# A hybrid decoder layer: the expert layers spread over the gate steps in another order, and chunk order at three stage borders

## The chip, the cores and the metric

The kernel runs on one core of a Trainium2 chip. The metric is the device time of one execution, in microseconds (us).

## What is computed

One decoder layer on 512 tokens of width 1024, in float32: two token mixers side by side (sparse attention and a state-space scan), a cross-attention to 256 memory tokens, and a PEER channel mixer, with a norm ahead of each. The change touches the cross-attention and PEER:

```python
h = h + merged @ w_out
h = h + memory_cross_attention(rmsnorm(h), rmsnorm(mem), w_cross_q, w_cross_kv, w_cross_out)
h = h + peer_ffn(rmsnorm(h), ...)
...
def peer_ffn(a, w_q, sub_keys, u_tab, v_tab):     # 8 heads, 128 keys a side, 16384 experts
    s = scores of both half queries against 128 sub keys
    s_top, i_top = top_k(s, 16)                   # per head and half
    sc, ci = top_k(all 256 sums, 16)              # 16 experts of each head
    gw = softmax(sc)
    act = gelu(a . u_tab[experts])
    return sum(gw * act * v_tab[experts])         # 128 experts a token
```

## The kernel before, in words

A tile framework records the program and a scheduler orders the instructions of each engine by their dependences, buffers and priorities. So the order on an engine is not the order of the code, and a tile's number of buffers decides how far loads and casts run ahead. All large products are made from a high and a low float32r part of each operand: `mm3` (L140) issues hi times hi, hi times lo for each of the eight chunks of the inner dimension, and then lo times hi for all chunks. `split` (L87) makes the parts: a cast on ScalarE (L90) and a subtraction (L91) on VectorE or GpSimd.

PEER runs for three blocks of 128 tokens (384, "dense") through all 16384 experts as 128 layers of 128 experts. Layer 1 (`layer1`, L890) is Gelu(uT a): 24 matmuls of 384 columns. Layer 2 (`layer2`, `sum_up`) multiplies by the gate weight of each token and expert and sums over vtab. The fourth block of tokens gathers its 128 experts' rows by indirect DMA on GpSimd (`gather_u`, `gather_v`; tile gr) and uses VectorE.

- *Choices* (`project` L949, `head` L968): for each of eight heads TensorE makes the scores (ps_q, ps_s) and VectorE the two rounds of top 16 with indices. `keep_some(n)` (L897) puts n layers of layer 1 between; their results, of which there are N_KEPT = 76, are stored to DRAM (gd) for later. `gather_some(P1G, h)` (L932) starts two gathers behind each block of a head and multiplies those started earlier.
- *Softmax* over the 16 scores of a head (L1046 to L1054), then eight layers (L1056).
- *Gate steps* (L1084 to L1115): 24 steps, eight for each of three blocks of tokens. `turned(b)` (L1062) transposes a block's chosen rows, columns and weights (ps_e). A step makes four one-hot operands on VectorE (oa, ob, obh, obl), 32 small matmuls (ps_w) that turn them into the gate weights of all 16384 experts for 16 tokens, four copies on ScalarE (stg) and a store to DRAM (wd). Behind the matmuls stands `keep_some`: two layers in the first two steps, one in the others.
- *Layer 2 stage*: gate weights (W) and the stored layer-1 results (gk) are loaded back, the rest of layer 1 is run, and yo is summed.

While the choices run, the weights of layer 1 are loaded into a ring of four buffers (cr), before and after into one of two (ur); the cast parts uh and ul have two buffers each. The loads stand on SP's queue, one behind another.

Of the kernel before, what the change touches and what calls it, by code (L numbers as in the profile page):

```python
# [21 lines left out]
T = 512  # L22
D = 1024
KC = 8
# [27 lines left out]
N_KEPT = 76  # L52
DENSE = 384
NTB = DENSE // 128
TG = 16
A8 = 8
P1G, P2G = 2, 0
NEARLY = 2
DELAY = 3


# [1 line left out]
def tile_hybrid(ctx, tc, xT, memT, pos, prm, cst, win, wab, wsb, wou, wcq, wckv, wco, wpq, subk, uT, utab, vtab,  # L63
# [73 lines left out]
                V.tensor_tensor(lo, raw, hi.bitcast(F32), op=OP.subtract)  # L137
        return hi, lo

    def mm3(ps, w, xh, xl, n=T, m=128, first=True, last=True, late_xl=False):  # L140

        hi, lo = w
        a, b, c = (hi, xh), (hi, xl), (lo, xh)
        order = [(*p, k) for k in range(KC) for p in (a, b)] + [(*c, k) for k in range(KC)]
        if late_xl:
            order = [(*p, k) for p in (a, c, b) for k in range(KC)]
        for i, (w_, x_, k) in enumerate(order):
            TE.matmul(ps[:m, :n], w_[:, k, :m], x_[:, k, :n], start=first and i == 0,  # L148
                      stop=last and i == len(order) - 1)
# [24 lines left out]
    def rsqrt_bc(ss, n, width):  # L174

        return bcast(rsqrt_small(const, ss[:, :n // 128], n // 128, 1.0 / width), n)
# [31 lines left out]
    ss = psum("ac", "ss")  # L208
# [499 lines left out]

    def mem_kv(m):
        ps = psum("mm", "ps_kv")  # L710
        mm3(ps, wtile(wckv[m], V if m < 12 else G), meH, meL, n=256)
        if m < 8:
            S.copy(kkT[:, m, :], ps[:, :256])
        else:
            vT = gen("vvT")[:, :256]
            S.copy(vT, ps[:, :256])
            ps2 = psum("sm", "ps_vv")
            for i in range(2):
                TE.transpose(ps2[:, i * 128:(i + 1) * 128], vT[:, i * 128:(i + 1) * 128], ident)
            V.tensor_copy(kkv[:, m - 8, 256:512], ps2[:, :256])  # L720
# [32 lines left out]
    for m in range(8):  # L753
        xr = gen("xr")
        SY.dma_start(xr, xT[:, m, :])
        ps = psum("mm", "ps_o")
        mm3(ps, wtile(wou[m]), mH, mL)
        V.tensor_tensor(h1[:, m, :], ps, xr, op=OP.add)
        S.activation(cH[:, m, :], h1[:, m, :], AF.Copy, scale=pc("g_cross", m))
        V.scalar_tensor_tensor(cL[:, m, :], h1[:, m, :], pc("g_cross", m), cH[:, m, :].bitcast(F32),  # L760
                               op0=OP.mult, op1=OP.subtract)
        if m < 7:
            add_square(sh, h1[:, m, :], T, m == 0)
        else:
            sum_small(ss, sh, T, True, False)
            sum_small(ss, square(h1[:, m, :], T), T, False, True)
    rs = wk.tile([128, T], F32, name="rs_c", bufs=1)
    S.copy(rs, rsqrt_bc(ss, T, D))

    for m in range(12, 14):  # L770
        mem_kv(m)


    xH, xL = slot2("xH", R), slot2("xL", R)
# [32 lines left out]
    sh = const.tile([128, T], F32, name="sh2", tag="rsf")  # L807
    for m in range(8):
        ps = psum("mm", "ps_h2")
        mm3(ps, wtile(wco[m]), xH, xL)  # L810
        V.tensor_tensor(h1[:, m, :], h1[:, m, :], ps, op=OP.add)
        if m < 7:
            add_square(sh, h1[:, m, :], T, m == 0)
        else:
            sum_small(ss, sh, T, True, False)
            sum_small(ss, square(h1[:, m, :], T), T, False, True)
# [152 lines left out]
    def head(h, sS, before):  # L969
# [3 lines left out]
        for b in order:  # L973
            for p in range(2):
                s = sS[:, p, b, :]
                V.max(out=tv[:, b, p, 0:8], in_=s)
                V.max_index(ti[:, b, p, 0:8], tv[:, b, p, 0:8], s)
                V.match_replace(out=s, in_to_replace=tv[:, b, p, 0:8], in_values=s, imm_value=TAKEN)
                V.max(out=tv[:, b, p, 8:16], in_=s)
                V.max_index(ti[:, b, p, 8:16], tv[:, b, p, 8:16], s)  # L980
            keep_some(2 if b == order[0] else 1)
            if b == order[0] and before is not None:
                decode(h - 1, *before)
            gather_some(P1G if h < 7 else 0, h)


        ca = sp.tile([128, 4, 64], F32, name="ca", tag="ca")
# [65 lines left out]
    V.tensor_tensor(sw, sw, top[:, :, None].to_broadcast([128, 32, 16]), op=OP.mult)  # L1053
    V.tensor_copy(gwt, slW[:, 3, :])  # L1054

    keep_some(8)  # L1056
    se1.close()
    choosing[0] = False
    vp = ctx.enter_context(tc.tile_pool(name="vp", bufs=1, side="right", reuse_waits="tile"))
# [21 lines left out]
        return eT  # L1081

    nxt = turned(0)
    for b in range(NTB):  # L1084
        eT = nxt
        for g in range(128 // TG):
# [13 lines left out]
            V.tensor_tensor(ob, io, bc(1), op=OP.is_equal)  # L1100
            V.tensor_tensor(obh, ob, bc(2), op=OP.mult)
            V.tensor_tensor(obl, ob, bc(3), op=OP.mult)
            for q in range(TG // 4):
                ps = psum("sm", "ps_w")
                for i in range(4):
                    w_ps, at_ = ps[:, i * 128:(i + 1) * 128], (slice(None), (q * 4 + i) // 2, slice(None), i % 2)
                    TE.matmul(w_ps, obh[at_], oa[at_], start=True, stop=False)  # L1107
                    TE.matmul(w_ps, obl[at_], oa[at_], start=False, stop=True)  # L1108
                S.activation(stg[:, :, q * 4:q * 4 + 4].rearrange("b a t -> b t a"),
                             ps.rearrange("b (t a) -> b t a", t=4), AF.Copy, scale=1.0 / 32768)  # L1110
            S.dma_start(wd[b * (128 // TG) + g], stg.rearrange("b a t -> b (a t)"))
            keep_some(2 if b * 8 + g < NEARLY else 1)
            gather_some(P2G)
    keep_some(N_KEPT)
    se2.close()  # L1115

# [221 lines left out]
```

## Time and profile before

| | before |
|---|---|
| median of 3 runs | 2165.53 us (2162.18 to 2165.95) |
| profiled execution | 2165.43 us |
| its span in the trace | 2163.7 us |
| TensorE busy | 2103.3 us (97% of the span) |
| VectorE busy | 1596.5 us (74%) |
| ScalarE busy | 977.6 us (45%) |
| GpSimd busy | 562.8 us (26%) |
| chain that ended last | PE 82%, DVE 12%, DMA 2%, ACT 2% |

The profiled execution lies by 1.7 us above its own span and within the runs. The names in the profile are PE (TensorE), PEld (its weight loads), DVE (VectorE), ACT (ScalarE), POOL (GpSimd) and SP. A busy share is an average over stages that are bound by different engines, so the stretches are read one by one below. A time in brackets behind a row is the idle time of the engine just before it, and what ended it.

### The profile page before, as it was taken

How to read it: one execution, taken by the hardware profiler on the slowest of the kernel's cores; microseconds unless marked ns; L12 is line 12 of the kernel's file. 1: busy time of each engine (PE TensorE's matmuls, PEld its weight loads, DVE VectorE, ACT ScalarE, POOL GpSimd, SP SyncE). 2: the span in 40 equal slices, each digit the busy share in tenths (PEclk: the TensorE clock that was granted, in tenths of full speed). 3: DMA queues.
4: the chain of work that ended last, by engine and by line, in shares of the span. 5: the costliest groups of instructions: out<-in, count | busy, mean ns of one | idle time of the engine just before them, and what ended most of it. 6: DMA issues, size and time to landing. Idle time of an engine off the chain costs nothing.

```text
span 2163.7 us, 29945 instructions
## 1 busy us (share of the span) xinstructions
PE 2103.3 (97%) x11045; PEld 1816.1 (84%) x11045; DVE 1596.5 (74%) x3018; ACT 977.6 (45%) x1513; POOL 562.8 (26%) x348
## 2 busy tenths in 40 slices
PE   9999999999999999999999999999999999999998
PEld 7888788777887877798988899988888888888887
DVE  6877855579943434589999588578778878788886
ACT  4453356666622434343434477633333333333333
POOL 0000000144134423214231000034344444444430
PEclk9999999999999999999999999999999999999999
DMA  4433332476453323258776376899999999999982
GB/s 138 136 108 116 104 103 83 126 209 181 143 165 103 121 68 107 98 168 308 262 240 223 130 259 257 287 329 370 324 331 337 336 354 327 350 319 332 339 304 79
DMA packets 209138, 469.27 MB, mean 217 GB/s; under 512 B 16064, under 2 KB 109376, under 8 KB 205792
## 3 DMA queue, kind: packets, MB, share of 16 engines
q1 hardware_dynamic: 152832, 284.10, 40.8%
q0 software_dynamic: 36864, 134.23, 16.8%
q10 hardware_dynamic: 19296, 49.03, 5.9%
q8 instruction: 86, 1.41, 0.3%
q14 instruction: 60, 0.49, 0.1%
HBM read 416.64 MB, written 50.66 MB: 216 GB/s over the span
## 4 chain that ended last, share of the span: by engine, by line
PE 82%; DVE 12%; DMA 2%; ACT 2%; issue 1%; POOL 0%; SPq 0%; DVEq 0%; ACTq 0%
PE yo L1144 24%; PE ps_u L148 19%; PE ps_in L148 16%; PE pss L148 4%; PE ps_cq L148 2%; PE ps_h L148 2%; DVE gr L908 2%; DVE ul L91 2%; PE ps_o L148 2%; PE psa L148 1%; PE ps_q L148 1%; PE ps_kv L148 1%; PE ps_w L1107 1%; PE ps_w L1108 1%; PE po L559 1%
## 5 line engine op out<-in xcount | busy, mean ns | idle before, releaser
L148 PE MATMUL ps_u<-fH,uh 128*128 128x384 f32 x1024 | 352.1, 344 | 12.0 <-ACT uh L90 12.0
L148 PE MATMUL ps_u<-fL,uh 128*128 128x384 f32 x1024 | 347.8, 340 | 0.0
L906 POOL DMA_INDIRECT gr<-utab,gidx x128 | 186.0, 1453 | 581.6 <-DVE gr L908 464.4
L91 POOL TENSOR_TENSOR wl<-wr,wh 128x1024 fp32r<-128x1024 f32 x60 | 148.1, 2469 | 661.5 <-PE ps_in L148 409.2
L919 POOL DMA_INDIRECT gr<-vtab,gidx x128 | 189.7, 1482 | 241.5 <-DVE acc L923 216.6
L90 ACT CAST vh<-vr 128x1024 fp32r<-128x1024 f32 x128 | 134.5, 1051 | 221.1 <-PE yo L1144 165.9
L90 ACT CAST wh<-wr 128x1024 fp32r<-128x1024 f32 x132 | 138.4, 1048 | 165.6 <-PE ps_in L148 78.5
L148 PE MATMUL ps_u<-fH,ul 128*128 128x384 f32 x1024 | 201.6, 338 | 8.2 <-DVE ul L91 8.0
L148 PEld LDWEIGHTS ps_u<-fH,uh 128*128 128x128 f32 x1024 | 196.4, 192 | 15.2 <-ACT uh L90 13.0
L148 PE MATMUL ps_in<-aH,wh 128*128 128x512 f32 x520 | 208.0, 400 | 0.0
L148 PE MATMUL ps_in<-aL,wh 128*128 128x512 f32 x520 | 204.7, 394 | 0.0
L1144 PE MATMUL yo<-vh,mh 128*128 128x512 f32 x768 | 199.8, 394 | 3.2 <-ACT mh L1134 3.2
L1144 PE MATMUL yo<-vh,ml 128*128 128x512 f32 x768 | 199.2, 393 | 0.0
L1144 PE MATMUL yo<-vl,mh 128*128 128x512 f32 x768 | 198.4, 392 | 0.0
L148 PEld LDWEIGHTS ps_u<-fL,uh 128*128 128x128 f32 x1024 | 196.4, 192 | 1.9
L91 DVE TENSOR_TENSOR vl<-vr,vh 128x1024 fp32r<-128x1024 f32 x128 | 156.6, 1225 | 55.1 <-ACT vh L90 44.2
L91 DVE TENSOR_TENSOR ul<-ur,uh 128x1024 fp32r<-128x1024 f32 x82 | 103.3, 1262 | 124.1 <-ACT uh L90 63.3
L148 PEld LDWEIGHTS ps_u<-fH,ul 128*128 128x128 f32 x1024 | 180.1, 189 | 12.7 <-DVE ul L91 12.7
L1144 PEld LDWEIGHTS yo<-vh,ml 128*128 128x128 f32 x768 | 145.1, 189 | 31.9
L1144 PEld LDWEIGHTS yo<-vl,mh 128*128 128x128 f32 x768 | 144.7, 188 | 31.8
L1144 PEld LDWEIGHTS yo<-vh,mh 128*128 128x128 f32 x768 | 144.2, 189 | 31.5 <-ACT mh L1134 3.5
L923 DVE SCALAR_TENSOR_TENSOR acc<-gr,gwt,acc 128x1024 f32<-128x1024 f32 x127 | 163.1, 1284 | 0.8
(472 smaller groups left out, 4066.5 us busy)
## 6 DMA issues: line engine op xcount, KB each, us to landing
vr<-vtab SPq DMA_DIRECT2D x128, 512.0 KB, 6.5
ur<-uT SPq DMA_DIRECT2D x80, 512.0 KB, 4.8
wr<-win SPq DMA_DIRECT2D x71, 512.0 KB, 3.6
cr<-uT SPq DMA_DIRECT2D x48, 512.0 KB, 4.3
wd<-stg ACTq DMA_DIRECT2D x24, 1024.0 KB, 4.0
W<-wd SPq DMA_DIRECT2D x16, 1536.0 KB, 14.3
gd<-ga ACTq DMA_DIRECT2D x76, 192.0 KB, 3.1
gk<-gd SPq DMA_DIRECT2D x76, 192.0 KB, 5.1
```

The lines of the kernel that those rows point to most:

```text
L90: made_hi[0] = S.copy(hi, src)
L91: return (lo_eng or V).tensor_tensor(lo, src, hi.bitcast(F32), op=OP.subtract)
L148: TE.matmul(ps[:m, :n], w_[:, k, :m], x_[:, k, :n], start=first and i == 0, stop=last and i == len(order) - 1)
L559: TE.matmul(po[:, b * 128:(b + 1) * 128], vt[:, s, (h // 4) * 128:(h // 4 + 1) * 128], pt[:, s * 128:(s + 1) * 128], start=s == 0, stop=s ...
L906: G.indirect_dma_start(out=r[:], out_offset=None, in_=utab[:, :], in_offset=bass.IndirectOffsetOnAxis(ap=gidx[:, k:k + 1], axis=0))
L908: return lambda: V.scalar_tensor_tensor(r, r, 1.0, afg, op0=OP.mult, op1=OP.mult, accum_out=gdot[:, k:k + 1])
L919: G.indirect_dma_start(out=r[:], out_offset=None, in_=vtab[:, :], in_offset=bass.IndirectOffsetOnAxis(ap=gidx[:, k:k + 1], axis=0))
L923: return lambda: V.scalar_tensor_tensor(acc, r, gwt[:, k:k + 1], acc, op0=OP.mult, op1=OP.add)
L1107: TE.matmul(w_ps, obh[at_], oa[at_], start=True, stop=False)
L1108: TE.matmul(w_ps, obl[at_], oa[at_], start=False, stop=True)
L1144: TE.matmul(yo[b][i], m[:, b * 128:(b + 1) * 128], v[:, i * 512:(i + 1) * 512], start=a == seq[0] and p == 0, stop=a == seq[-1] and p == 2)
```

## The change

Four things change.

1. `mm3` gets `late_k`: the three products of one chunk stand together, chunk by chunk. It is used for the first output block of three products: the memory keys, the output projection and the cross output.
2. Behind the cross norm's sum, one memory product (`mem_kv(12)`) stands between the inverse root and its broadcast.
3. No gathers are started behind the last block of a head in the choices; instead one is started in every second gate step.
4. Behind the softmax stands one layer instead of eight (`LAST1`), then the first transposes. In each gate step the layers stand ahead of the matmuls of the one-hots: two in the first step, then 29 spread over 23 steps (one each, two in six of them). Four layers stand behind the last step (`LAST2`).

```diff
@@ -54,8 +54,8 @@
 NTB = DENSE // 128
 TG = 16
 A8 = 8
-P1G, P2G = 2, 0
-NEARLY = 2
+P1G = 2
+LAST1, LAST2 = 1, 4
 DELAY = 3
 
 
@@ -137,13 +137,15 @@
                 V.tensor_tensor(lo, raw, hi.bitcast(F32), op=OP.subtract)
         return hi, lo
 
-    def mm3(ps, w, xh, xl, n=T, m=128, first=True, last=True, late_xl=False):
+    def mm3(ps, w, xh, xl, n=T, m=128, first=True, last=True, late_xl=False, late_k=False):
 
         hi, lo = w
         a, b, c = (hi, xh), (hi, xl), (lo, xh)
         order = [(*p, k) for k in range(KC) for p in (a, b)] + [(*c, k) for k in range(KC)]
         if late_xl:
             order = [(*p, k) for p in (a, c, b) for k in range(KC)]
+        if late_k:
+            order = [(*p, k) for k in range(KC) for p in (a, b, c)]
         for i, (w_, x_, k) in enumerate(order):
             TE.matmul(ps[:m, :n], w_[:, k, :m], x_[:, k, :n], start=first and i == 0,
                       stop=last and i == len(order) - 1)
@@ -708,7 +710,7 @@
 
     def mem_kv(m):
         ps = psum("mm", "ps_kv")
-        mm3(ps, wtile(wckv[m], V if m < 12 else G), meH, meL, n=256)
+        mm3(ps, wtile(wckv[m], V if m < 12 else G), meH, meL, n=256, late_k=m == 0)
         if m < 8:
             S.copy(kkT[:, m, :], ps[:, :256])
         else:
@@ -754,7 +756,7 @@
         xr = gen("xr")
         SY.dma_start(xr, xT[:, m, :])
         ps = psum("mm", "ps_o")
-        mm3(ps, wtile(wou[m]), mH, mL)
+        mm3(ps, wtile(wou[m]), mH, mL, late_k=m == 0)
         V.tensor_tensor(h1[:, m, :], ps, xr, op=OP.add)
         S.activation(cH[:, m, :], h1[:, m, :], AF.Copy, scale=pc("g_cross", m))
         V.scalar_tensor_tensor(cL[:, m, :], h1[:, m, :], pc("g_cross", m), cH[:, m, :].bitcast(F32),
@@ -765,10 +767,10 @@
             sum_small(ss, sh, T, True, False)
             sum_small(ss, square(h1[:, m, :], T), T, False, True)
     rs = wk.tile([128, T], F32, name="rs_c", bufs=1)
-    S.copy(rs, rsqrt_bc(ss, T, D))
-
-    for m in range(12, 14):
-        mem_kv(m)
+    y = rsqrt_small(const, ss[:, :4], 4, 1.0 / D)
+    mem_kv(12)
+    S.copy(rs, bcast(y, T))
+    mem_kv(13)
 
 
     xH, xL = slot2("xH", R), slot2("xL", R)
@@ -807,7 +809,7 @@
     sh = const.tile([128, T], F32, name="sh2", tag="rsf")
     for m in range(8):
         ps = psum("mm", "ps_h2")
-        mm3(ps, wtile(wco[m]), xH, xL)
+        mm3(ps, wtile(wco[m]), xH, xL, late_k=m == 0)
         V.tensor_tensor(h1[:, m, :], h1[:, m, :], ps, op=OP.add)
         if m < 7:
             add_square(sh, h1[:, m, :], T, m == 0)
@@ -981,7 +983,7 @@
             keep_some(2 if b == order[0] else 1)
             if b == order[0] and before is not None:
                 decode(h - 1, *before)
-            gather_some(P1G if h < 7 else 0, h)
+            gather_some(P1G if h < 7 and b != order[-1] else 0, h)
 
 
         ca = sp.tile([128, 4, 64], F32, name="ca", tag="ca")
@@ -1053,7 +1055,7 @@
     V.tensor_tensor(sw, sw, top[:, :, None].to_broadcast([128, 32, 16]), op=OP.mult)
     V.tensor_copy(gwt, slW[:, 3, :])
 
-    keep_some(8)
+    keep_some(LAST1)
     se1.close()
     choosing[0] = False
     vp = ctx.enter_context(tc.tile_pool(name="vp", bufs=1, side="right", reuse_waits="tile"))
@@ -1081,6 +1083,7 @@
         return eT
 
     nxt = turned(0)
+    kept_then = kept[0] + 1
     for b in range(NTB):
         eT = nxt
         for g in range(128 // TG):
@@ -1100,6 +1103,14 @@
             V.tensor_tensor(ob, io, bc(1), op=OP.is_equal)
             V.tensor_tensor(obh, ob, bc(2), op=OP.mult)
             V.tensor_tensor(obl, ob, bc(3), op=OP.mult)
+
+            at = b * (128 // TG) + g
+            if at == 0:
+                keep_some(2)
+            else:
+                step = (N_KEPT - LAST2 - kept_then) / (NTB * 128 // TG)
+                keep_some(int((at + 1) * step) - int(at * step))
+            gather_some(at % 2)
             for q in range(TG // 4):
                 ps = psum("sm", "ps_w")
                 for i in range(4):
@@ -1109,8 +1120,6 @@
                 S.activation(stg[:, :, q * 4:q * 4 + 4].rearrange("b a t -> b t a"),
                              ps.rearrange("b (t a) -> b t a", t=4), AF.Copy, scale=1.0 / 32768)
             S.dma_start(wd[b * (128 // TG) + g], stg.rearrange("b a t -> b (a t)"))
-            keep_some(2 if b * 8 + g < NEARLY else 1)
-            gather_some(P2G)
     keep_some(N_KEPT)
     se2.close()
 
```

The line numbers of the new program are 2 to 11 higher from the output projection on. What the scheduler makes of it, at three places:

PE, from the end of the layers behind the choices to the first one-hot products. The rows are the last matmuls of a layer (ps_u), the transposes (ps_e) of the chosen rows, columns and weights, and the first product (ps_w). Before:

```order
L148 MATMUL ps_u<-fH,ul 128x384 x8
L1068 MATMUL ps_e<-cs,slA 128x128
L1068 MATMUL ps_e<-cs,slB 128x128
L1068 MATMUL ps_e<-cs,slW 128x128
L1107 LDWEIGHTS obh
L1107 MATMUL ps_w<-oa,obh 128x128
```

and now:

```order
L150 MATMUL ps_u<-fH,ul 128x384 x8
L1070 MATMUL ps_e<-cs,slA 128x128
L1070 MATMUL ps_e<-cs,slB 128x128
L1070 MATMUL ps_e<-cs,slW 128x128
L150 MATMUL ps_u<-fH,uh 128x384
L150 MATMUL ps_u<-fL,uh 128x384
```

Ahead of the transposes there were 18 layers behind the last scores, and now there are 11; between the transposes and the first product there was none, and now there are two layers (48 matmuls).

ACT, at the border from the first block of tokens to the second. Here stg is the copy of the products, wd its store, uh the cast of a layer's weights, ga the Gelu behind a layer, gd its store. Before (from the eighth step's store on):

```order
L90 CAST uh<-ur 128x1024
L1111 DMA wd<-stg 128x2048
L894 ACTIVATE ga<-ps_u 128x384
L1109 ACTIVATE stg<-ps_w 128x4x128
L900 DMA gd<-ga 128x384
L1109 ACTIVATE stg<-ps_w 128x4x128 x3
L894 ACTIVATE ga<-ps_u 128x384
L1111 DMA wd<-stg 128x2048
L900 DMA gd<-ga 128x384
L1109 ACTIVATE stg<-ps_w 128x4x128 x4
L90 CAST uh<-ur 128x1024
```

and now (from the seventh step's store on):

```order
L90 CAST uh<-ur 128x1024
L1122 DMA wd<-stg 128x2048
L896 ACTIVATE ga<-ps_u 128x384
L90 CAST uh<-ur 128x1024
L902 DMA gd<-ga 128x384
L896 ACTIVATE ga<-ps_u 128x384
L90 CAST uh<-ur 128x1024
L902 DMA gd<-ga 128x384
L1120 ACTIVATE stg<-ps_w 128x4x128 x4
L1122 DMA wd<-stg 128x2048
```

Before, the Gelu of the last layer that has been cast and four copies stand ahead of the next cast; this occurs twice in the 24 steps. Now a cast stands behind every Gelu or every group of copies, and at every place one cast layer more than the finished ones has been issued.

SP, from the loads of the last layers to the first read of the gate weights (W). Before:

```order
L876 DMA cr<-uT 128x1024 x18
L876 DMA ur<-uT 128x1024 x26
L1124 DMA vr<-vtab 128x1024 x3
L876 DMA ur<-uT 128x1024
L1159 DMA gf<-gfin 128x1024
L1149 DMA W_12835<-wd 128x24x128
```

and now:

```order
L878 DMA cr<-uT 128x1024 x11
L878 DMA ur<-uT 128x1024 x33
L1133 DMA vr<-vtab 128x1024 x2
L1168 DMA gf<-gfin 128x1024
L878 DMA ur<-uT 128x1024
L1158 DMA W_12833<-wd 128x24x128
```

Seven loads moved from the ring of four buffers to the ring of two, and one load of layer-2 rows (vr) from ahead of W to behind it. Of the gathers' products on DVE, 48 stood ahead of the softmax, and 46 still do: the scheduler takes ten of the twelve that the code moves to gate steps forward into the choices. The order on POOL is the same in both.

## Rows read from the trace of the kernel before

**Rows 1.** Windows: length, busy of PE, PEld, DVE, ACT, POOL; clock, DMA share, GB/s.

```profile
961.00:1184.00 223.00, 212.02 (x1125) 197.51 (x1124) 217.35 (x850) 90.00 (x115) 74.91 (x55) 0.98 0.77 260
...
1417.00:2134.00 717.00, 717.00 (x3424) 626.19 (x3423) 574.08 (x727) 269.16 (x357) 300.82 (x201) 1.00 0.92 326
```

**Rows 2.** TensorE's waits, 961 to 1420: us in total, times, longest.

```profile
PE ps_u L148 <- ACT uh L90: 12.0, 4, 4.0
PE ps_u L148 <- DVE ul L91: 8.0, 9, 2.6
PE ps_w L1107 <- DVE obh L1101: 5.4, 1, 5.4
PE yo L1144 <- ACT mh L1134: 3.2, 1, 3.2
```

**Rows 3.** Busy time in stretches of the gate steps; columns as in rows 1.

```profile
1217.00:1238.00 21.00, 15.60 (x118) 14.87 (x117) 19.55 (x21) 8.22 (x11) 0.00 (x0) 0.84 0.39 133
1248.00:1285.00 37.00, 37.00 (x346) 36.17 (x343) 34.73 (x34) 30.87 (x37) 0.00 (x0) 1.00 0.76 275
1285.00:1303.00 18.00, 13.99 (x100) 13.50 (x99) 12.48 (x11) 10.15 (x12) 0.00 (x0) 0.81 0.62 226
...
1340.00:1358.00 18.00, 14.26 (x121) 13.77 (x119) 12.40 (x12) 10.49 (x13) 0.00 (x0) 0.91 0.68 242
1389.00:1418.00 29.00, 24.37 (x117) 22.19 (x116) 12.64 (x15) 14.40 (x19) 0.00 (x0) 0.88 0.99 357
...
1223.00:1229.00 6.00, 6.00 (x40) 5.69 (x41) 5.96 (x6) 3.77 (x4) 0.00 (x0) 0.50 0.01 3
```

**Rows 4.** The chain that ended last, two neighbouring steps: start, us, what.

```profile
1254.37 4.22 PE ps_u L148 x24
1260.45 4.22 PE ps_u L148 x24
```

**Rows 5.** Timeline of DVE at the first products: start, us, engine, instruction [idle before].

```profile
1217.34 1.23 DVE L91 TENSOR_TENSOR ul<-ur,uh 128x1024 fp32r<-128x1024 f32 x1 [2.94 <-PE ps_e L1068]
...
1222.81 1.22 DVE L1102 TENSOR_TENSOR obl<-ob,wll 128x2048 f16<-128x2048 f16 x1
```

**Rows 6.** Timeline of ACT at the first chunk border.

```profile
1290.59 3.70 ACT L1109 ACTIVATE stg<-ps_w 128x512 f32<-128x512 f32 x4 [0.74 <-PE ps_w L1108]
1294.08 1.05 ACT L90 CAST uh<-ur 128x1024 fp32r<-128x1024 f32 x1
```

**Rows 7.** Border to layer 2: one row of the chain, then timelines (q: a queue).

```profile
1388.89 12.27 PE ps_u L148 x71
...
1391.31 0.33 ACTq L1111 DMA_DIRECT2D wd<-stg  x1
...
1400.69 0.38 SPq L1149 DMA_DIRECT2D W<-wd  x1
...
1402.85 0.44 PE L148 MATMUL ps_u<-fH,uh 128*128 128x384 f32 x1 [1.42 <-ACT uh L90]
...
1410.52 0.79 PE L1144 MATMUL yo<-vh,mh 128*128 128x512 f32 x1 [3.21 <-ACT mh L1134]
```

**Rows 8.** Groups of DVE instructions, 961 to 1184: busy, mean ns | idle before.

```profile
L908 DVE SCALAR_TENSOR_TENSOR gr<-gr,afg 128x1024 f32<-128x1024 f32 x48 | 58.2, 1222 | 5.2 <-DMA gr<-utab,gidx 5.2
```

**Rows 9.** Timeline of PE behind the softmax's exponential.

```profile
1178.09 0.69 PE L148 MATMUL ps_u<-fH,uh 128*128 128x384 f32 x1 [2.79 <-ACT uh L90]
```

**Rows 10.** Timelines of the output projection and the cross-attention border.

```profile
696.57 5.88 DVE L746 SCALAR_TENSOR_TENSOR mL<-th,mH 128x512 fp32r<-128x512 f32 x6
...
697.51 0.39 PE L148 MATMUL ps_o<-mH,wh 128*128 128x512 f32 x1
...
697.81 2.88 POOL L91 TENSOR_TENSOR wl<-wr,wh 128x1024 fp32r<-128x1024 f32 x1 [3.05 <-PE pss L148]
...
701.30 0.50 PE L148 MATMUL ps_o<-mL,wh 128*128 128x512 f32 x1 [1.59 <-DVE mL L746]
...
752.54 1.13 PE L181 MATMUL ps_rs<-cs,rq_i 128*128 128x128 f32 x8 [2.34 <-DVE rq_i L104]
```

## The prediction, made before the changed kernel was run

> **What bounds the kernel now.** I read the page first, then busy time by stage, then TensorE's waits, then single stretches in the timeline. The page gives TensorE 97% of the span, so the question is where its few idle microseconds lie. By stage [rows 1]: the long last stage (layer 2, from 1417) has none, 717.00 busy of 717.00, so what this change does there can give nothing. The choices stage (961 to 1184) leaves 223.00 - 212.02 = 10.98 us idle with VectorE busy for 217.35 of 223: VectorE sets its pace. Between them lie the gate steps and the border to layer 2; the waits table [rows 2] names four kinds of wait from 961 to 1420, 28.6 us in all.
>
> Each wait costs more than its idle time. The granted clock is 0.50, the 1.2 GHz level, from 1223 to 1229, behind the longest one, and 1.00 (2.4 GHz) from 1248 to 1285, where TensorE never waited [rows 3]. So I price a stall as the idle time of its window plus (1 - mean clock) times the window, less 0.6 us where the low stretch may begin inside the idle time (a choice; 0.3 at the last). From [rows 3]:
> - first one-hot products: 21.00 - 15.60 = 5.40 idle, 0.16 x 21 = 3.4, less 0.6: **8.2 us**;
> - first chunk border: 18.00 - 13.99 = 4.01 idle, 0.19 x 18 = 3.4, less 0.6: **6.8**;
> - second chunk border: 3.74 idle, 0.09 x 18 = 1.6: **5.4**;
> - border to layer 2: 29.00 - 24.37 = 4.63 idle, 0.12 x 29 = 3.5, less 0.3: **7.8**.
> Together 28.2 us. An undisturbed gate step (one layer and its products) takes 1260.45 - 1254.37 = 6.08 us, of which the layer is 4.22 [rows 4] and the products 1.86; to this the disturbed stretches can fall.
>
> **The change part by part.**
> *First products.* Before, the three transposes are followed at once by products. These need VectorE's chain: from the weight split at 1217.34 to the end of the last product operand, 1222.81 + 1.22 = 1224.03, it takes 6.7 us [rows 5]. The new order puts two layers, 8.4 us, between the transposes and the products and leaves VectorE's chain as it was. 8.4 covers 6.7, so I take the gain as 8.2. Bounds: 5.4 (only the idle time goes) to 8.2.
>
> *Chunk borders.* ScalarE copied out four product tiles (3.70 us from 1290.59) and only then cast the next layer's weights (1294.08) [rows 6]; TensorE stood for 4.0 us [rows 2]. In the order before, no cast is ahead of TensorE at these two places. In the new order one always is, since layers stand in front of the products. Gain 6.8 + 5.4 = 12.2; 7.7 if the idle time goes and the low clock stays. I take 12.2: with no wait there is no reason for the low clock in [rows 3].
>
> *Steps of two layers.* The number of layers is the same. Seven loads go from the four-deep ring (cr) to the two-deep one (ur), and six steps have two layers in a row: 2 x 4.22 + 1.86 = 10.3 us of TensorE. ScalarE has 30.87 us of work in six single steps [rows 3], 5.1 each; a second layer adds a cast (1.05, [rows 6]) and a shorter Gelu pass, so under 7.3, which fits. The waits on the split are 8.0 us in nine [rows 2], 0.9 each; I let two of the pairs pay that: cost 1.8. Bounds: 0 to 7 (about one wait of each pair).
>
> *Border to layer 2.* The last product ended at 1388.9; its copy left for DRAM at 1391.31, the read of the weights was issued at 1400.69, and the first layer-2 product started at 1410.52 [rows 7], 21.6 us after the last product. TensorE had four layers to run meanwhile, 16.9 us; now it has five, 21.1. On SP two loads of layer-2 rows instead of three stand ahead of the weight read. That leaves 0.5 us bare. The 1.42 us wait for a layer load that came late [rows 7] may stay in part. I take 6.5 of the 7.8; bounds 2 (both waits stay) to 7.8.
>
> *Choices.* The diff takes 12 gathers out of heads 1 to 6, but the scheduler pulls ten of them forward again: 46 of 48 gather products still stand ahead of the softmax. GpSimd's order is the same in both. Two fewer, at 1.22 us each [rows 8], give 2.4 on the bounding engine. The wait of 2.79 us at 1178.09 [rows 9] is for a cast behind the exponential and its two table loads; now one more cast stands ahead of them, a layer's 4.2 us of cover. But VectorE is busy to the end of the stage, so I let TensorE profit by 1.9. Together 4.3; bounds -2 (one more wait of the size of this one in a new VectorE order, and nothing won) to 9 (most of the 10.98 idle).
>
> *Borders of earlier stages.* At the output projection VectorE's six low-part operations took 5.88 us while GpSimd's weight split lay beside one of them, from 697.81 for 2.88; TensorE ran nine matmuls from 697.51 and then waited 1.59 us, to 701.30 [rows 10]. That is (701.30 - 1.59 - 697.51) / 9 = 0.24 a matmul. With the three products of a chunk taken together, 13 fit ahead of the same low part: 4 x 0.24 = 0.9 us (my reading; from 0 to 1.59). The Trainium skill, "SBUF — State Buffer", section "Who interferes with whom", says that a VectorE instruction with two SBUF inputs and a GpSimd instruction that reads SBUF shut each other out for a whole instruction. The rows agree with it. By that rule the stretched operation stays and 0.9 is what is won; without it the whole 1.59 could go, and the sum would be 0.7 larger. At the cross-attention border TensorE waited 2.34 us for the normalisation [rows 10]; there the change puts one matmul and two transposes more ahead of the wait: 0.3, and 0.3 at the next projection. Sum 1.5; bounds -1 to 2.5.
>
> **Sum**: 8.2 + 12.2 - 1.8 + 6.5 + 4.3 + 1.5 = 30.9 us. The profiled execution took 2165.43 us (1.7 of it around the span), 0.1 under the median of 2165.53. 2165.4 - 30.9 = 2134.5; I say **2134**. With every term at its poor end it is 2165.4 - (5.4 + 7.7 - 7 + 2 - 2 - 1) = 2160; at its good end 2165.4 - (8.2 + 12.2 + 7.8 + 9 + 2.5) = 2126.
>
> **The rivals.**
> *The border to layer 2 keeps its waits (0.17).* A chain of copy, store, weight read and multiply remains there, and a layer load that lands late stops TensorE as at 1402.85 [rows 7]. For it: nothing in the change shortens that chain. Against it: one more layer of cover. Losing the 6.5 and paying at four pair steps instead of two (1.8 more) gives 2134.5 + 8.3 = 2143; with low clock behind each, up to 2147.
> *The choices really loosen (0.06).* If the products of all 12 gathers, 14.7 us, left VectorE's share of the choices, what remains of the idle time, 10.98 - 2.79 = 8.2 us, could go: 2126. The order speaks against it.
> *Slower: the pairs starve (0.04).* The second layer of each pair finds its cast stuck behind four copies, as at the chunk border, because the two-deep ring gave it its load late. One such stall cost 6.8 us; six cost 41, more than the 30.9 won: 2134 + 41 = 2175. From five such stalls (34) the kernel is slower. Against it: the single steps use the same ring, and from 1248 to 1285 TensorE never waited [rows 3].
> *Nothing comes of it (0.03).* The waits come back elsewhere in the same size: 2165.
>
> **How the numbers follow.** The forecast has 0.70 (2126 to 2141). With the first rival the range is **2126 to 2147**. About 0.2%, 4.3 us, is what a measurement can tell from no change. Faster by more: 0.70 + 0.17 + 0.06 = 0.93; within it 0.03; slower 0.04.
>
> **What would show it.** Right: no wait of products on VectorE's operand behind the transposes; no 4 us wait on a cast in the gate steps and clock 1.00 through them; pairs of layers without idle time; under 2 us idle at the border to layer 2; the choices still paced by VectorE and some 4 us shorter. Wrong: waits on the cast at pair steps, longer choices, or a layer-2 stage that is no longer 717 us of solid work.

## The result, and the profile after

The changed kernel took 2140.54 us in the median of 5 runs (2139.56 to 2142.68), the kernel before 2164.23 beside it (2162.18 to 2165.95). The ratio is 0.9891, 95% interval 0.9878 to 0.9903: 23.7 us faster, inside the range of the prediction and 0.77 of the gain that it forecast. The span of the profiled execution fell from 2163.7 to 2139.6 us, by 24.1.

Where these 24.1 us come from shows when both traces are cut at the first or last matmul of a tile. Layers that moved from one piece to another are taken out at 4.18 us each (24 matmuls, some 174 ns apart).

| piece, from one mark to the next | before | after | layers moved | difference | forecast |
|---|---|---|---|---|---|
| start to first memory key (ps_kv) | 570.65 | 569.96 | | -0.7 | |
| to the first scan projection (pss) | 39.56 | 42.55 | | **+3.0** | 0 |
| to the last output projection (ps_o) | 133.01 | 133.05 | | 0.0 | -0.9 |
| to the first query (ps_cq) | 12.05 | 13.90 | | **+1.85** | -0.3 |
| to the last scores (ps_s) | 378.22 | 378.50 | | +0.3 | -2.7 |
| to the first transposes (ps_e) | 83.58 | 50.16 | -7 | -4.2 | -1.9 |
| to the last one-hot product (ps_w) | 171.60 | 177.86 | +6 | **-18.8** | -18.6 |
| to the first layer-2 product (yo) | 21.85 | 23.30 | +1 | -2.7 | -6.5, both |
| to the end | 753.13 | 750.30 | | -2.8 | |

The gate steps and the border to layer 2 gave what was forecast. The borders of the earlier stages were forecast to win 1.5 us and lost over 4 in this pair of executions; how much of that the change caused is taken up below.

The windows of the changed kernel (columns as in rows 1): the choices, the gate steps, the border to layer 2, and the layer-2 stage.

```profile
965.00:1188.00 223.00, 212.69 (x1147) 196.54 (x1147) 216.40 (x847) 91.46 (x116) 71.02 (x53) 1.00 0.73 250
1188.00:1366.00 178.00, 176.52 (x1523) 172.24 (x1522) 149.86 (x142) 131.66 (x156) 0.00 (x0) 1.00 0.76 264
1366.00:1395.00 29.00, 27.06 (x151) 25.66 (x149) 13.66 (x16) 15.59 (x21) 1.76 (x1) 1.00 0.96 344
1417.00:2130.00 713.00, 713.00 (x3395) 621.45 (x3394) 569.72 (x735) 267.72 (x360) 295.44 (x197) 1.00 0.90 319
```

The gate steps now have 1.48 us of idle time in 178, at full clock; before, three windows in them had clocks of 0.84, 0.81 and 0.91 [rows 3]. The border to layer 2 is down from 4.63 us idle to 1.94 in a window of the same 29 us, with no low clock. The layer-2 stage is still solid. VectorE still paces the choices.

TensorE's waits from the choices to the first layer-2 products (as rows 2):

```profile
PE ps_u L150 <- DVE ul L91: 8.8, 11, 1.6
PE yo L1153 <- ACT mh L1143: 1.8, 1, 1.8
PE ps_u L150 <- DVE e L1073: 1.1, 1, 1.1
PE ps_u L150 <- ACT uh L90: 1.0, 1, 1.0
PE ps_u L150 <- ACT stg L1120: 0.3, 1, 0.3
PE ps_u L150 <- issue: 0.3, 1, 0.3
```

The 12.0 us of waits on a cast have become 1.0, the 5.4 us on the product operand are gone, and 3.2 ahead of layer 2 have become 1.8. The 8.8 us on the split lie in the choices as before.

How the first products are covered now: the last rows of VectorE's chain, and TensorE's first product.

```profile
1188.39 1.22 DVE L91 TENSOR_TENSOR ul<-ur,uh 128x1024 fp32r<-128x1024 f32 x1 [1.64 <-PE ps_e L1070]
...
1193.87 1.22 DVE L1105 TENSOR_TENSOR obl<-ob,wll 128x2048 f16<-128x2048 f16 x1
...
1196.80 0.24 PE L1118 MATMUL ps_w<-oa,obh 128*128 128x128 f16 x1
```

The chain takes 6.7 us again (1188.39 to 1195.09) and ends 1.7 us before TensorE comes, as worked out from rows 5.

And the place that lost: ScalarE and TensorE at the third and fourth memory key, changed kernel. Here wh is the cast of a weight, yH a scaling, kkv the copy of a finished key.

```profile
578.59 0.71 ACT L703 ACTIVATE yH<-xs,pr 128x512 fp32r<-128x512 f32 x1
579.20 0.35 ACT L715 COPY kkv<-ps_kv 128x256 f32<-128x256 f32 x1
579.45 1.34 ACT L703 ACTIVATE yH<-xs,pr 128x512 fp32r<-128x512 f32 x2
580.69 1.03 ACT L90 CAST wh<-wr 128x1024 fp32r<-128x1024 f32 x1
...
581.78 0.93 PE L150 MATMUL ps_kv<-meHL,wh 128*128 128x256 f32 x5 [2.57 <-ACT wh L90]
```

The same stretch of ScalarE before:

```profile
577.97 1.14 ACT L154 ACTIVATE sq<-xs 128x512 f32<-128x512 f32 x2
579.01 1.03 ACT L90 CAST wh<-wr 128x1024 fp32r<-128x1024 f32 x1
579.94 0.37 ACT L713 COPY kkv<-ps_kv 128x256 f32<-128x256 f32 x1
```

Before, the cast stands ahead of the copy of the third key. Now the copy, which waits for that key's last matmul, and two scalings stand ahead of the cast, and TensorE waits 2.57 us for it. No edit touches this line: the chunk order of the first key alone (`late_k=m == 0`) made the scheduler order ScalarE anew, as the kernel with only this line undone shows below. The clock is low in this piece too: 0.5 from 582.4 to 585.8.

### The profile page after: what moved, and what is told of

Same layout as the page of the kernel before. It is cut to its first block, busy times and chain, and to the rows that moved or that the text cites. A ratio compares the mean times of both kernels' runs of the same rounds, so it can differ in the third digit from the quotient of the medians.

```text
span 2139.6 us, 29944 instructions
## 1 busy us (share of the span) xinstructions
PE 2091.2 (98%) x11045; PEld 1803.9 (84%) x11045; DVE 1594.0 (74%) x3018; ACT 976.1 (46%) x1513; POOL 564.1 (26%) x348
## 4 chain that ended last, share of the span: by engine, by line
PE 62%; DVE 9%; DMA 1%; issue 1%; ACT 0%; POOL 0%; SPq 0%; DVEq 0%; ACTq 0%
PE yo L1153 24%; PE ps_u L150 19%; PE pss L150 4%; PE ps_q L150 2%; PE ps_cq L150 2%; PE ps_h L150 2%; DVE ul L91 2%; PE ps_kv L150 2%; PE ps_o L150 1%; DVE gr L910 1%; PE ps_w L1118 1%; PE ps_w L1119 1%; PE ps_co L805 1%; PE ps_cl L787 1%; DMA gk<-gd 1%
## 5 line engine op out<-in xcount | busy, mean ns | idle before, releaser
L150 PE MATMUL ps_u<-fH,uh 128*128 128x384 f32 x1024 | 346.4, 338 | 2.6 <-DVE e L1073 1.1
L150 PE MATMUL ps_u<-fL,uh 128*128 128x384 f32 x1024 | 342.6, 335 | 0.0
L91 DVE TENSOR_TENSOR ul<-ur,uh 128x1024 fp32r<-128x1024 f32 x89 | 110.8, 1247 | 111.0 <-ACT uh L90 71.3
```

The costliest lines, as they stand in the source:

```text
L91: return (lo_eng or V).tensor_tensor(lo, src, hi.bitcast(F32), op=OP.subtract)
```

## The experiments

Each kernel ran beside the kernel before; ratios are to it. The single kernels differ by a few us, so the verdicts rest on the pieces of the trace as well as on the times.

**The borders undone.** In the changed kernel:

```diff
-        mm3(ps, wtile(wckv[m], V if m < 12 else G), meH, meL, n=256, late_k=m == 0)
+        mm3(ps, wtile(wckv[m], V if m < 12 else G), meH, meL, n=256)
...
-        mm3(ps, wtile(wou[m]), mH, mL, late_k=m == 0)
+        mm3(ps, wtile(wou[m]), mH, mL)
...
-    y = rsqrt_small(const, ss[:, :4], 4, 1.0 / D)
-    mem_kv(12)
-    S.copy(rs, bcast(y, T))
-    mem_kv(13)
+    S.copy(rs, rsqrt_bc(ss, T, D))
+    for m in range(12, 14):
+        mem_kv(m)
...
-        mm3(ps, wtile(wco[m]), xH, xL, late_k=m == 0)
+        mm3(ps, wtile(wco[m]), xH, xL)
```

> The changed kernel with the first and second part of the change undone: no chunk order in the three first blocks, and the broadcast of the root ahead of both memory products as before. Theory 1 (these parts cost time: from the first memory-key product to the first product of the scan's output projection the changed kernel takes 3.0 us longer, from the last output-projection product to the first query product 1.85 us longer, and wins only 0.7 ahead of them): the time falls by about 4.2 us, to some 2136.3, and the low-clock stretches behind both places are gone. Rival (the longer borders come from something else in the program, such as the gathers or the layers, or differ from one execution to the next): the time stays at 2140.5 within 1 us.

Measured: 2139.06 us, ratio 0.9893 (0.9874 to 0.9913). The memory keys took 39.92 us instead of 42.55 and the piece to the first query 12.31 instead of 13.90, 4.2 us less in the two pieces as theory 1 says. But the memory keys began 2.0 us later than in the changed kernel, in a part that no edit touches, and the time fell by 1.5 us only, the ratio (0.9893 against 0.9891) not at all. In the times it is nearer to the rival; in the pieces it is theory 1. The next three runs part them.

**Only the first memory key undone** (the first two lines of the diff above).

> The changed kernel with the chunk order undone at the first memory-key product alone. Theory 1 (chunk order there makes the scheduler put two more of ScalarE's scaling operations ahead of the fourth weight cast, and TensorE stands 2.6 us for that cast, with low clock behind it): the wait goes, 3.0 us are won there and 0.7 are lost at the start of the memory keys: about 2138.2. Rival (the order of ScalarE comes from elsewhere): the 2.6 us wait stays, 2140.5 or 0.7 more.

Measured: 2137.18 us, ratio 0.9877 (0.9857 to 0.9898), and 39.81 us for the memory keys: 2.7 less than in the changed kernel. The waits in its memory keys:

```profile
PE ps_kv L150 <- ACT wh L90: 0.7, 2, 0.5
PE ps_vv L721 <- ACT vvT L718: 0.3, 1, 0.3
```

The 2.57 us wait is gone. Theory 1 holds for it: all nine kernels of this study with this chunk order have a wait of 2.5 to 2.7 us on that cast, and in the kernel before and the four runs without it no such wait is longer than 0.5. The 2.7 us are not all the chunk order's, though. In six of the nine the keys took 41.0 to 41.6 us at full clock, in the other three, the changed kernel among them, 42.6 to 43.8 with a stretch of low clock; without the chunk order they took 39.5 to 39.9, at full clock each time. So the order costs 1.1 to 2.1 us, and a low clock that follows only in some kernels makes it 2.6 to 4.3. What the order wins at the start of the keys (0.7 in the theory) can't be read: the start moves by more than that between executions of one kernel.

**Only the root's broadcast moved back** (the third part of the diff).

> The changed kernel with the broadcast of the root again ahead of both memory products. Theory 1 (the move causes the 1.85 us at the cross-attention border): about 2138.7. Rival (the move wins its 0.3 us of wait, 2.0 instead of 2.34, and the 1.85 comes from the waits just ahead of it, the squares that come 0.35 later and the low clock that follows; these are there with or without the move): no change or up to 0.5 us slower, 2140.5 to 2141, with the low clock still behind the border.

Measured: 2141.2 us, ratio 0.9900 (0.9879 to 0.9920). The piece took 13.49 us, with the low clock still in it. This is the rival's picture: the wait for the normalisation is 2.3 us again instead of the changed kernel's 2.0, and the low clock has another cause than the move.

**Only the output projection undone** (the second part).

> The changed kernel with the chunk order undone at the output projection alone. Theory 2 (chunk order there wins nothing, since the first block still ends with the last chunk's high part, 8.05 against 8.02 us behind the last scan product; and the low clock at the cross-attention border goes with it: it was there in the four kernels with this order and absent in the two without): the border is 1.3 to 1.6 us shorter without low clock, about 2139. Rival (the low clock there depends on something else): border unchanged, 2140.5.

Measured: 2140.48 us, ratio 0.9881 (0.9865 to 0.9898); the piece to the first query took 14.40 us, low clock and all. Theory 2 falls in its second half. Its first half stands: the piece of the output projections did not change in any kernel, 45.7 us with and without the chunk order.

**The same kernel a second time** (as the kernel with only the first memory key undone).

> The changed kernel with the chunk order undone at the first memory key alone, for a second time and with more rounds, as the measure for the run beside it: 2137 again, 2 to 3 us under the changed kernel.

Measured: 2140.16 us, ratio 0.9879 (0.9862 to 0.9897). The before kernel was slower beside it, too, so the ratio is the same as at first. By the ratios this kernel is some 3 us faster than the changed one both times; each interval still overlaps that of the changed kernel. The two profiles of this one kernel, 740 to 765 us, first and second execution:

```profile
740.00:765.00 25.00, 22.52 (x128) 19.69 (x127) 8.19 (x19) 7.91 (x11) 10.05 (x5) 0.93 0.31 95
```

```profile
740.00:765.00 25.00, 22.51 (x134) 19.57 (x133) 8.79 (x19) 7.74 (x11) 11.57 (x5) 1.00 0.31 100
```

The same instructions with the same 2.5 us of idle time run at clock 0.93 in one execution and at 1.00 in the other, and the piece from the last output projection to the first query took 13.0 and 12.05 us. So the low clock there comes and goes with the change in place. In the four executions with the whole border change and full clock the piece took 11.86 to 12.15 us, against 12.05 in the kernel before: nothing of the 1.85 us is left. Whether the change makes the low clock more frequent stays open. Eight of the twelve executions with all or part of the border change had it, and neither of the two without.

**The gathers back in the choices.**

```diff
-            gather_some(P1G if h < 7 and b != order[-1] else 0, h)
+            gather_some(P1G if h < 7 else 0, h)
...
-            gather_some(at % 2)
+            gather_some(0)
```

> The changed kernel with the gathers as before, two behind every block of heads 0 to 6 in the choices and none in the gate steps. Theory (of the 12 products moved, only two left the choices, and VectorE's order there is what counts): within 1 us of 2140.5, to either side, and the choices as long as in the changed kernel. Rival (the predicted 2.4 us were won, and lost again to something else in the choices): about 2143.

Measured: 2145.47 us, ratio 0.9918 (0.9897 to 0.9939): both numbers were too small. TensorE's order is the same as in the changed kernel. Most is lost in one piece: from the last scores to the transposes 54.69 us instead of 50.16. Another 1.6 us are lost behind the first layer-2 product, with a stretch of low clock that the changed kernel did not have. Its waits from 1134 to 1190 us, and then those of the changed kernel:

```profile
PE ps_u L150 <- ACT uh L90: 2.8, 1, 2.8
PE ps_u L150 <- DVE ul L91: 2.1, 1, 2.1
```

```profile
PE ps_u L150 <- DVE ul L91: 1.6, 3, 1.1
PE ps_u L150 <- ACT uh L90: 1.0, 1, 1.0
```

The 2.8 us wait behind the exponential [rows 9] is back. So moving the gathers removed it: in the changed kernel VectorE's last choices end 46.5 us behind the last scores, here 50.4, and ScalarE's exponential, with the cast behind it, comes that much earlier. Two products fewer are 2.4 us of these 3.9; where the rest comes from is not shown. Idle time makes up 2.3 of the 4.5 us; the rest goes with two stretches of low clock, from 1148.9 and 1179.6, that the kernel before has at the same two waits and the changed kernel not. The prediction put this wait down to an additional cast ahead of the table loads, and paid the gathers separately. The next kernel bears the gathers out: it has eight layers ahead of the transposes again, with the gathers moved, and its waits here are the changed kernel's.

**Eight layers ahead of the transposes, the rest ahead of the products.**

```diff
-LAST1, LAST2 = 1, 4
+LAST1, LAST2 = 8, 4
```

> The changed kernel with eight layers instead of one between the softmax and the transposes, as before; the layers still stand ahead of the products, but there are only about 24 of them for 24 steps (two in the first, then one in nearly each). Theory (it is the place ahead of the products that removes the waits, and one layer a step is enough; the wait behind the exponential is removed by the gathers, not by this): no wait of products on their operands, no 4 us wait on a cast, no 2.8 us wait behind the exponential: 2140.5 within 1.5. Rival (the seven layers had to move into the steps to keep a cast ahead of the copies): one or two waits of 4 us come back, 2147 to 2153.

Measured: 2158.32 us, ratio 0.9963 (0.9951 to 0.9976): 18 us of the gain gone (16 by the ratio), more than even the rival said. TensorE's waits from 1180 us on:

```profile
PE ps_u L150 <- ACT uh L90: 8.9, 3, 3.8
PE yo L1153 <- ACT mh L1143: 4.6, 1, 4.6
PE ps_e L1070 <- DVE e L1073: 1.7, 1, 1.7
PE ps_u L150 <- DVE e L1073: 1.3, 1, 1.3
```

Layers stand ahead of the products here, and still TensorE waits twice for 3.7 us as at the chunk borders before, in ScalarE's order of before:

```profile
1276.06 0.49 ACT L896 ACTIVATE ga<-ps_u 128x384 f32<-128x384 f32 x1 [1.75 <-PE ps_u L150]
...
1277.01 3.69 ACT L1120 ACTIVATE stg<-ps_w 128x512 f32<-128x512 f32 x4 [0.46 <-PE ps_w L1119]
1280.52 1.04 ACT L90 CAST uh<-ur 128x1024 fp32r<-128x1024 f32 x1
...
1281.61 0.69 PE L150 MATMUL ps_u<-fH,uh 128*128 128x384 f32 x1 [3.73 <-ACT uh L90]
```

A Gelu, four copies, and only then the cast.

**Six layers behind the last step** (so 27 in the last 23 steps, not 29).

```diff
-LAST1, LAST2 = 1, 4
+LAST1, LAST2 = 1, 6
```

> The changed kernel with six layers instead of four kept behind the last gate step. Theory (the first layer-2 product waits 1.8 us for the weights' read-back, which two more layers of 4.2 us would cover): the wait goes, about 2138.5. Rival (behind the last products the DMA queues are nearly full, and more layer loads there delay the read-back or the layers themselves): the wait stays or becomes a wait on a layer's load, 2140 to 2144.

Measured: 2149.36 us, ratio 0.9921 (0.9904 to 0.9937). The wait ahead of layer 2 is gone as expected, but the time rose by 9 (7 by the ratio): in the steps there is again a wait for a cast in two places.

```profile
PE ps_u L150 <- ACT uh L90: 5.7, 2, 3.6
```

Neither theory had this; two layers fewer in the steps were enough.

**The same layers behind the products.**

```diff
-            at = b * (128 // TG) + g
...
-            gather_some(at % 2)
             for q in range(TG // 4):
...
             S.dma_start(wd[b * (128 // TG) + g], stg.rearrange("b a t -> b (a t)"))
+            at = b * (128 // TG) + g
...
+            gather_some(at % 2)
```

> The changed kernel with the same layers (and gathers) put behind the products of each step instead of ahead of them. Theory (the order within the step is what the 18.8 us between the first transposes and the last products come from): the 5.4 us wait behind the transposes and waits of about 4 us where a step follows without a cast in hand come back with their low clock: 2153 to 2161. Rival (the spreading of 1.25 layers a step does it, in whichever place): only the first wait comes back, about 2149.

Measured: 2145.04 us, ratio 0.9907 (0.9891 to 0.9924). Of all waits, only the first comes back:

```profile
PE ps_w L1111 <- DVE obh L1104: 5.4, 1, 5.4
PE ps_w L1111 <- DVE e L1073: 0.9, 1, 0.9
```

The rival is right. The place ahead of the products is worth the first wait and the low clock behind it; it does nothing for the waits at the chunk borders. These go by ScalarE's order. In the orders of three kernels, the one before and those with LAST1 = 8 and with LAST2 = 6, a longer run of steps of one layer each ends in a step whose Gelu and copies have no cast ahead: all layers that were cast are finished. This occurs twice in each of the three, at the waits, and nowhere with two layers in every fourth step, in front of the products or behind them.

**One operation of VectorE less in each step** (on the kernel with LAST1 = 8).

```diff
-            V.tensor_tensor(obl, ob, bc(3), op=OP.mult)
+            obl = obh
```

> The kernel with eight layers ahead of the transposes and one a step (last1_8), with one of VectorE's four operations of every gate step left out: the low part of the second one-hot operand (obl) is not made, and the products use the high part twice. TensorE and ScalarE have the same work, VectorE 24 x 1.22 = 29 us less. Theory 3 (what stops TensorE in the steps is ScalarE's order: at two places no cast is ahead, and the next one stands behind a Gelu and four copies; these places are in the order of this kernel too, one step later): the two waits of about 4 us stay, and the time is within 4 us of the 2158.3 of last1_8. Rival (VectorE, which has nearly as much work in a step of one layer as TensorE, is what TensorE falls behind): the waits go, 2145 or less.

Measured: 2157.26 us, ratio 0.9959 (0.9945 to 0.9973). The kernel leaves out the low part of the second one-hot operand. With 29 us less work for VectorE the two waits are still there, of 4.03 and 3.77 us (the third is behind the last step), the first a step later, as the order has it.

```profile
PE ps_u L150 <- ACT uh L90: 9.2, 3, 4.0
```

VectorE's work is not what they come from.

**The next layer's cast written ahead** (on the same kernel).

```diff
-                S.dma_start(gd[kept[0]], layer1(kept_at[kept[0]], "sm"))
+                k = kept[0]
+                parts = ahead.pop() if ahead else None
+                if parts is None:
+                    parts = wtile(uT[kept_at[k]], "u")
+                if not choosing[0] and k + 1 < N_KEPT:
+                    ahead.append(wtile(uT[kept_at[k + 1]], "u"))
+                ps = psum("sm", "ps_u")
+                mm3(ps, parts, fH, fL, n=DENSE)
...
```

> The kernel with eight layers ahead of the transposes and one a step (last1_8), with the load and the cast of each next layer written ahead of the layer before it. TensorE's, VectorE's and ScalarE's work is the same as in last1_8; in ScalarE's order a cast is now ahead in every step. Theory 3 (ScalarE's order): the two waits of nearly 4 us in the steps and the low clock behind them go, 2158.3 less 8 to 12, about 2148; the 4.6 us wait ahead of the first layer-2 product may stay. Rival (VectorE's share of a step): the waits stay as waits on a split or an operand, 2155 or more.

Measured: 2150.06 us, ratio 0.9924 (0.9907 to 0.9941), 8 us less by the order alone. The waits on a cast within the steps are gone; the one left (3.3) is behind the last step. Now the transposes wait for VectorE:

```profile
PE ps_e L1081 <- DVE e L1084: 5.5, 3, 2.5
PE ps_u L150 <- ACT uh L90: 3.3, 1, 3.3
PE yo L1164 <- ACT mh L1154: 1.6, 1, 1.6
```

So theory 3 holds for the two waits, and the rival has a part in the rest: with one layer a step VectorE is nearly as long as TensorE (34.73 of 37.00 us, [rows 3]), and its additional operations for the next block show at once. Steps of 1.25 layers cure both: in its steps the changed kernel has 1.1 us of waits on these rows and none on a cast.

**One layer more behind, one fewer ahead of the transposes**, on the kernel with the first key undone.

```diff
-LAST1, LAST2 = 1, 4
+LAST1, LAST2 = 0, 5
```

> The changed kernel with the chunk order undone at the first memory key, and one layer moved from ahead of the transposes to behind the last step (LAST1, LAST2 = 0, 5); the density in the steps stays 1.25. If the 1.8 us wait of the first layer-2 product is a lack of cover, it goes, and the transposes wait up to 1 us for VectorE: 2136, some 1 us under the run of the same kernel with 1, 4 beside it. Rival (the fifth layer's load is late on the full queues, or VectorE is later than read): the same or 1 to 3 us more.

Measured: 2136.75 us, ratio 0.9865 (0.9848 to 0.9881), against 2140.16 for the kernel with 1, 4 beside it. The intervals overlap, so the times alone do not part them. The trace shows no wait ahead of layer 2 any more and shows the transposes not waiting for the choices. From the last scores to the first layer-2 product it takes 250.3 us, against 251.3 to 252.3 in the changed kernel and the five runs with the same steps and gathers. Its waits from 1180 us on:

```profile
PE ps_u L150 <- DVE e L1073: 1.1, 1, 1.1
PE ps_e L1070 <- ACT stg L1120: 0.6, 1, 0.6
PE ps_u L150 <- ACT stg L1120: 0.6, 1, 0.6
```

It has the lowest ratio of all kernels that ran, that of the changed kernel included (0.9891, 0.9878 to 0.9903).

## Why the prediction was right, and where it was wrong

*First products*: forecast 8.2 us. The wait went, as the two layers cover VectorE's chain. With the layers behind the products it is back with 5.4 us and a low clock behind it, and that kernel is 7.6 us longer from the first transposes to the last one-hot product (layers taken out). So the 8.2 is about right. On the whole it lost only 5.2, since the two layers of its last step stand behind the products, cover the read of the gate weights and win 2.4 there.

*Chunk borders*: forecast 12.2, and with the first products and the pairs together 18.6 against 18.8 measured. The size was right and the reason given was wrong. "Layers stand in front of the products" does not put a cast ahead; that is shown by the kernel with layers in front and the waits there (LAST1 = 8), and by the one with layers behind and no waits. Two layers in every fourth step do it, or a cast written ahead. That the size came out is not luck alone: the new order of ScalarE, with a cast ahead at these borders, had been read before the run. Only why it is so was guessed. As a general rule the order does not put a cast behind every Gelu or group of copies: early in the steps two casts stand together and two groups of copies follow. What counts is that a cast is ahead.

*Steps of two layers*: forecast to cost 1.8; the waits in the steps sum up to 1.4 (1.1 on the transposed rows, 0.3 on a copy), none of them 0.9 on the split. The rival of starving pairs was the wrong way round: pairs are what keeps the casts ahead.

*Border to layer 2*: forecast 6.5, measured 2.7 + 2.8 = 5.5, the first of them idle time, the second the low clock that went. The wait that stays is 1.8 instead of the 0.5 worked out; another layer of cover removes it.

*Choices*: forecast 4.3, measured 4.2 less 0.3. The sum is right, in part by luck; the split into two terms is not. Up to the last scores nothing was won. The gathers won it all behind the last scores, by shortening two waits from 4.8 to 2.6 us, one of them the wait that the prediction credited to a cast. The other 2 us are low clock behind these two waits, which the prediction did not price in this stage.

*Borders of earlier stages*: forecast to win 1.5, within -1 to 2.5; they lost 4.2 in the profiled pair. This is the step that failed. First, the prediction said nothing of the memory keys, where one changed line moved a cast behind a copy and two scalings: 1.1 to 2.1 us at full clock, 3.0 in the profiled pair with a stretch of low clock. Second, at the output projection the row of 1.59 us was not the limit of its stage. The changed kernel there:

```profile
702.54 0.39 PE L150 MATMUL ps_o<-mH,wh 128*128 128x512 f32 x1
...
703.63 0.50 PE L150 MATMUL ps_o<-mL,wh 128*128 128x512 f32 x1 [0.71 <-DVE mL L748]
...
706.83 0.50 PE L150 MATMUL ps_o<-mH,wh 128*128 128x512 f32 x1 [1.08 <-ACT mH L747]
```

The wait for the low part falls from 1.59 to 0.71, by the 0.9 forecast, and 1.08 us of a new wait follow: the first block reaches the last chunk, whose high part is ready 7.2 us behind the last scan product in either kernel (704.44 and 706.77). The block ends 8.05 us behind it instead of 8.02. The stretched VectorE operation is still there: 2.89 us beside GpSimd's split of 2.91, where its neighbours take 0.7. The Trainium skill, "SBUF — State Buffer", section "Who interferes with whom", has it that a VectorE instruction with two SBUF inputs contends with a GpSimd instruction that reads SBUF, and the trace agrees. That neither 0.9 nor 1.59 was won has the reason just given. Third, the 1.85 us at the cross-attention border go with a low clock that comes and goes between executions of one program. At full clock the border is as long as before, though the wait for the normalisation fell by the forecast 0.3 (2.34 to 2.0). The 0.3 at the next projection is not seen either: TensorE's waits from the first query to the choices (1.5, 0.7 and 0.6 us) are the same in both kernels.

What makes the wait for the normalisation long was overlooked. In the kernel before:

```profile
749.02 2.37 POOL L91 TENSOR_TENSOR wl<-wr,wh 128x1024 fp32r<-128x1024 f32 x1 [2.89 <-PE ps_kv L148]
749.10 2.31 DVE L102 TENSOR_TENSOR rq_q<-rq_i 128x4 f32<-128x4 f32 x1
...
751.84 0.16 DVE L102 TENSOR_TENSOR rq_q<-rq_i 128x4 f32<-128x4 f32 x1
```

A VectorE operation on four columns in the chain of the inverse root takes 2.31 us beside a GpSimd split of 2.37, and 0.16 without one. It is the same in the changed kernel (2.32 beside 2.38). No run moved that split, so what this would win is open.

The difference of 6.8 us between forecast (30.9) and profiled gain (24.1) is thus 5.7 for the borders, 1.0 for the border to layer 2 and 0.4 for the choices, less 0.2 for the steps and 0.1 of rounding. Of the 5.7, the change's own are the 1.5 not won and the 1.1 to 2.1 at the memory keys; the rest is low clock and the scatter of the start. Two side sums of the prediction are loose, without effect on its forecast: the 2126 of the rival on the choices counts the 2.4 us of the gathers twice (2128.7 without), and six pairs at 0.9 us each make 5.4, not the 7 of the bound.

## What to carry to other kernels

Where one engine serves two streams in order, ask at every place of the issue order how many operands of the next large piece are ready ahead; a place with none costs the whole of what stands in between, whichever engine has time to spare. When work is spread to fill a stage, give the leading engine clearly more of it in each step than the others have; here 1.25 layers a step instead of 1 was worth over 15 us, of which some 8 could be had by the order of the casts alone, and 1.17 gave nearly half of it back. Where a scheduler orders the code, compare its order at every place a line touches, also for edits that look harmless, and cut the wait that ends last, not the first one in the row.

## What the runs showed of the hardware that was not expected

The granted clock fell to 0.5 (the 1.2 GHz level) not only behind long waits. From about 753 us it fell in one execution of a kernel and not in another, with the same waits of 0.5 and 2.0 us before it; over all kernels that piece took 13.0 to 14.4 us with the low clock and 11.9 to 12.3 without. The memory keys with their wait of 2.5 to 2.7 us had a low clock in three kernels of nine. The start of the memory keys, which no part of the change is ahead of, moved between 568.6 and 573.2 us over all executions, and from 570.2 to 572.25 between the two of one kernel. So a single profile of this kernel places a gain only to some 2 us, unless the piece and the clock in it are looked at by themselves.
